# Layer 0's feed-forward input products as seven products of halves, the residual summed in DRAM, some low parts made on GpSimd

## The chip, the cores and the metric

One core of a Trainium2 chip runs the whole program. The metric is device time in microseconds (us) of one execution; several executions are taken and their median is given. The engines are TensorE (PE in the profile, its weight loads PEld), VectorE (DVE), ScalarE (ACT), GpSimd (POOL) and SyncE (SP, which here only issues transfers). POOL issues transfers too.

## The reference

One inference step of two layers over 640 tokens (512 latent, 128 context), model width 1024, in float32. Layer 0 mixes by attention, layer 1 by a bidirectional mLSTM; each mixer is followed by a SwiGLU feed-forward block with 2816 hidden columns. Shift, scale and gate of every block come from a product of the conditioning with `w_ada`. What the change touches is the feed-forward block:

```python
D_MODEL = 1024
D_FF = 2816

def modulate(x, g, shift, scale):
    return rms_norm(x, g) * (1.0 + scale) + shift

def swiglu(h, w_in, w_out):
    a, b = jnp.split(h @ w_in, 2, axis=-1)
    return (jax.nn.silu(a) * b) @ w_out

for l in range(2):
    ...                       # mixer: x = x + gate1 * mixer(modulate(x, ...))
    x = x + gate2 * swiglu(modulate(x, g_ffn[l], shift2, scale2), w_ffn_in[l], w_ffn_out[l])
y = rms_norm(x, g_final)
```

## The kernel before

**Numbers in two parts.** Every float32 operand of a large product is split into a high part (`hi`, rounded to the fp32r type) and a low part (`lo` = value - `hi`). A product is then three passes: high by high, high by low, low by high. ACT makes the high parts (`S.copy`), DVE the low parts (`V.tensor_tensor(... subtract)`).

**Weights.** `wspecs` lists all weight blocks in the order of use. `wload` takes the next one and starts its transfer into a buffer of the tag `raw` (four of them, shared with the modulation weights), `wprep` makes `whi` on ACT and `wlo` on DVE (five buffers each), `take` hands a pair to a product, `done` lets the next loads and preparations go. So weights are prepared up to five blocks ahead.

**Feed-forward, layer 0 (`ffn`).** For each of 22 blocks of 128 hidden columns PE makes `ffa` and `ffb` (the two halves of `h @ w_in`): 8 chunks of the model width x 3 passes x 2 halves of the tokens = 48 matmuls of 320 columns each, so 96 for a block. ACT and DVE make silu(a) * b and its high and low part `gh`, `gl`. Blocks go in groups (`GROUPS`: 8, 8, 6); after each group `ffn_out` multiplies the group's columns with `w_ffn_out` (tiles `fo`, 5 token tiles x 2 halves of the width) and `residual` adds gate * product onto x, which stays in SBUF.

**Feed-forward, layer 1 (`ffn7`).** The product of two 2 x 2 block matrices is made with seven products in place of eight. A unit is two blocks of 128 columns; the token dimension is halved (320 and 320), the model width too (512 and 512). The input appears in seven forms (`f1`, `f2`, `t1`, `t2`, `t3`, `f3`, `t4`: sums and differences of halves, class `Forms`), the weights in seven (steps 0 to 6; step 2 and step 4 load a block and add another onto it by an accumulating transfer of POOL's queue, steps 3 and 5 add on DVE). A unit is 7 products of 24 matmuls; results `X`, `Y`, `Z`, `W` (tiles `ffx`, `ffy`, `ffz`, `ffw`) are added into a and b on DVE. `put` writes the high and low parts of silu(a) * b into `g`. Units go in groups of 3, 3, 3 and 2, each followed by `ffn_out`.

**Modulation.** The product with `w_ada` for later blocks is made on DVE in the background: `ada_gen` loads a block of `w_adaT` (`araw`) and makes two dots (`junk`, L264, one for the latent and one for the context conditioning). `half_ada` is one dot, `bg_ada(1)` two. `ADA_FFN` says how many go after each block of layer 0's feed-forward. 160 dots in all.

**Order.** Each engine works through its instructions in program order, as the scheduler of the language laid them out; waits are semaphores. All tiles of one `tag` share their buffers.

Of the kernel before, what the change touches and what calls it, by code (L numbers as in the profile page):

```python
# [17 lines left out]
NT = 5  # L18
# [8 lines left out]
ADA_FFN = [0] + [2] * 8 + [1] * 13  # L27
# [18 lines left out]
GROUPS = [(0, 8), (8, 16), (16, 22)]  # L46


SEVEN = {1}
GROUPS7 = [(0, 6), (6, 12), (12, 18), (18, 22)]  # L50
# [3 lines left out]
def order7(d0, d1):  # L54

    us = range(d0 // 2, d1 // 2)
    steps = [(u, n) for u in us for n in range(7)]
    if d0 == 0:
        first = [(u, n) for u in (0, 1) for n in (0, 1)]
        steps = first + [s for s in steps if s not in first]  # L60
    return steps
# [8 lines left out]
def _build(ctx, tc, nc, A):  # L70
# [10 lines left out]
    xs_dram = dp.tile([TOK, 1024], F32, name="xs_dram", tag="xs")  # L81
    m_dram = dp.tile([64, TOK], F32, name="m_dram", tag="md")
# [63 lines left out]
    stp = cp.tile([128, 2, 2, 2, 3, 129], F32, name="stp", tag="stp")  # L146
    G.memset(stp.rearrange("p a e d k c -> p (a e d k c)"), 0.0)


    def wspecs():  # L150
# [11 lines left out]
        for l in range(2):  # L162
# [7 lines left out]
            for d0, d1 in GROUPS7 if l in SEVEN else GROUPS:  # L170
                if l in SEVEN:
                    st = {u: {"u": A["ffs"][u], "own": u != 1} for u in range(d0 // 2, d1 // 2)}
                    for u, step in order7(d0, d1):
                        yield st[u], step
                else:
                    for d in range(d0, d1):
                        for ab in range(2):
                            yield A["ffi"][l, d][:, ab]
                for half in range(2):
                    yield from chunk(A["ffo"][l, half][:, d0:d1, :], d1 - d0)  # L180
# [5 lines left out]
    ready = []  # L186
    live = [0]

    def wload():
# [4 lines left out]
        if isinstance(src, tuple):  # L194
# [3 lines left out]
            if first:  # L198

                raw = st[step] = (cp.tile([128, 2, 4, 128], F32, name=nm("wr"), tag=f"cB{step}") if step < 2 and st["own"] else  # L200
                                  Wp.tile([128, 2, 4, 128], F32, name=nm("wr"), tag="raw", bufs=4))
                SP.dma_start(raw, st["u"][first])
# [5 lines left out]
        SP.dma_start(raw, src)  # L208
# [3 lines left out]
    def wprep(n=99):  # L212
        for _ in range(min(n, len(raws))):
            if n == 99 and live[0] - len(raws) >= HELD:
                break
            raw = raws.pop(0)
# [10 lines left out]
            V.tensor_tensor(out=lo, in0=raw, in1=hi.bitcast(F32), op=ALU.subtract)  # L227
# [245 lines left out]
    class Forms:  # L473
# [14 lines left out]
        def split(self, name, f, cols, neg=False):  # L488
# [24 lines left out]
        def second(self, f, g, cols):  # L513
# [21 lines left out]
    def ffn7(l, x, forms, norm_last, bg, gate_fn, tile_done):  # L535
        gate = None
# [21 lines left out]
        def put(s, b, i, half):  # L558
            V.tensor_tensor(out=s, in0=s, in1=b, op=ALU.mult)
            for c, n, o in ((0, 256, 256 * half), (256, 64, 512 + 64 * half)):  # L560
# [3 lines left out]
                V.tensor_tensor(out=lo, in0=src, in1=hi.bitcast(F32), op=ALU.subtract)  # L564
# [15 lines left out]
        def step(u, n, i):  # L580
            w = units.setdefault(u, {})
            if n == 0:
                w["X"] = one("ffx")
                product(w["X"][0], 0, True, False)
                if u == 0:
                    norm_last()
                w["a1"] = T(640, "a1")
                S.copy(v2(w["a1"]), w["X"][1][0][1])
            elif n == 1:
                Y = two("ffy")  # L590
                product(Y[0], 1, True)
                a1 = w.pop("a1")
                add(a1, a1, Y)
# [16 lines left out]
            elif n == 5:  # L610
# [3 lines left out]
                put(silu(a2), w.pop("b2"), i, 1)  # L614
            else:
# [1290 lines left out]
```

## Time and profile before

| what | us |
|---|---|
| median of 3 runs | 1640.87 (1639.44 to 1643.06) |
| profiled execution, its own time | 1635.13 |
| its span, first to last instruction | 1633.4 |
| PE busy / DVE / ACT / POOL | 1592.5 / 1112.0 / 747.7 / 181.6 |
| layer 0's mixer up to its second half | 0 to 376 |
| second half of its output product | 376 to 399.5 |
| feed-forward of layer 0 | 399.5 to 870 |
| mLSTM mixer of layer 1 | 870 to 1165 |
| second half of its output product | 1165 to 1190.5 |
| feed-forward of layer 1 | 1190.5 to 1633.4 |

The stages are cut where the first matmul of a stage starts. The span is what the engines did in one execution; the execution's own time has some 1.7 us around it.

### The profile page before, as it was taken

The page shows a single profiled execution, that of the slowest core. Times are in us where ns is not written, and L with a number is a line of the kernel's source. Part 1 is how long each engine was busy: PE and PEld are TensorE (multiplying, and loading weights), DVE is VectorE, ACT ScalarE, POOL GpSimd, SP SyncE. Part 2 cuts the span into 40 slices and gives each one's busy share as a digit, 9 for nine tenths or more (in the row PEclk, how much of TensorE's full clock was granted, in tenths as well). Part 3 has the DMA queues.
Part 4 walks back from the last instruction along what each step waited for, and adds up shares of the span by engine and source line. Part 5 has one row for each costly group of instructions (what it writes and reads, how often), then busy time and mean ns, then how long its engine had stood idle before and what let it go on. Part 6 is the DMA issues. An engine that isn't in the chain of part 4 may idle for free.

```text
span 1633.4 us, 24402 instructions
## 1 busy us (share of the span) xinstructions
PE 1592.5 (97%) x9434; PEld 1447.0 (89%) x9434; DVE 1112.0 (68%) x1924; ACT 747.7 (46%) x1546; POOL 181.6 (11%) x213
## 2 busy tenths in 40 slices
PE   8999999999999999999999999989999999999997
PEld 7877898788999799979989998988789899899896
DVE  7687888866665565435557638598698677577567
ACT  5442558946432133213336234666476245155153
POOL 0001103420000000000000002663100100000000
PEclk8999999999999999999999999989999999999999
DMA  8354030043444343313324516452436554364331
GB/s 330 144 175 158 31 101 26 5 153 98 133 150 143 99 160 113 107 52 129 117 94 139 172 50 203 158 152 92 110 104 162 130 131 140 78 168 130 79 102 65
DMA packets 60900, 199.38 MB, mean 122 GB/s; under 512 B 7696, under 2 KB 10512, under 8 KB 60784
## 3 DMA queue, kind: packets, MB, share of 16 engines
q1 hardware_dynamic: 52736, 170.84, 32.6%
q0 software_dynamic: 7904, 26.79, 7.1%
q8 instruction: 74, 1.21, 0.3%
q14 instruction: 42, 0.34, 0.1%
q10 hardware_dynamic: 144, 0.20, 0.0%
HBM read 191.09 MB, written 6.71 MB: 121 GB/s over the span
## 4 chain that ended last, share of the span: by engine, by line
PE 87%; DVE 5%; ACT 4%; DMA 2%; issue 1%; POOL 0%; SPq 0%; DVEq 0%; POOLq 0%; ACTq 0%
PE ffa L343 9%; PE ffb L343 9%; PE fo L323 6%; PE fo L321 6%; PE fo L322 6%; PE ffw L546 5%; PE ffx L546 5%; PE ffz L546 4%; PE qk L343 3%; PE ffy L546 2%; PE in L321 2%; PE in L323 2%; PE in L322 2%; PE s L1133 2%; PE vo L323 2%; PE vo L322 2%
## 5 line engine op out<-in xcount | busy, mean ns | idle before, releaser
L226 ACT CAST whi<-wr 128x1024 fp32r<-128x1024 f32 (+2 forms) x228 | 235.2, 1034 | 539.9 <-PE fo L323 150.9
L227 DVE TENSOR_TENSOR wlo<-wr,whi 128x1024 fp32r<-128x1024 f32 (+2 forms) x228 | 275.0, 1212 | 147.5 <-ACT whi L226 145.4
L264 DVE SCALAR_TENSOR_TENSOR junk<-araw,cB 128x1024 bf16<-128x1024 f32 x160 | 194.8, 1245 | 28.6 <-DMA araw<-w_adaT 28.4
L456 DVE TENSOR_TENSOR tmp<-fo,g 128x512 f32<-128x512 f32 (+1 forms) x71 | 48.4, 682 | 110.3 <-PE fo L323 100.5
L321 PE MATMUL fo<-whi,hh 128*128 128x512 f32 x220 | 88.2, 401 | 0.0
L323 PE MATMUL fo<-whi,hl 128*128 128x512 f32 x220 | 87.9, 399 | 0.0
L323 PE MATMUL fo<-whi,g 128*128 128x512 f32 (+1 forms) x224 | 86.9, 390 | 0.0
L322 PE MATMUL fo<-wlo,g 128*128 128x512 f32 (+1 forms) x224 | 86.9, 388 | 0.0
L322 PE MATMUL fo<-wlo,hh 128*128 128x512 f32 x220 | 86.7, 394 | 0.0
L321 PE MATMUL fo<-whi,g 128*128 128x512 f32 (+1 forms) x224 | 86.6, 387 | 0.0
L343 PE MATMUL ffa<-hh,whi 128*128 128x320 f32 (+1 forms) x352 | 82.0, 310 | 0.0
L343 PE MATMUL ffa<-hl,whi 128*128 128x320 f32 (+1 forms) x352 | 81.8, 310 | 0.0
L343 PE MATMUL ffa<-hh,wlo 128*128 128x320 f32 (+1 forms) x352 | 81.5, 309 | 0.0
L343 PE MATMUL ffb<-hh,whi 128*128 128x320 f32 (+1 forms) x352 | 81.1, 308 | 0.2 <-ACT hh L375 0.2
L343 PE MATMUL ffb<-hl,whi 128*128 128x320 f32 (+1 forms) x352 | 80.7, 307 | 0.3 <-DVE hl L376 0.3
L343 PE MATMUL ffb<-hh,wlo 128*128 128x320 f32 (+1 forms) x352 | 80.5, 306 | 0.0
L546 PE MATMUL ffx<-form,whi 128*128 128x320 f32 x352 | 78.0, 309 | 0.0
L546 PE MATMUL ffz<-form,whi 128*128 128x320 f32 x352 | 78.0, 308 | 0.0
L1081 ACT ACTIVATE P<-s,s 128x640 f32<-128x640 f32 (+1 forms) x80 | 56.9, 712 | 33.4 <-DVE s L1076 29.1
L322 PE MATMUL vo<-wlo,hh 128*128 128x384 f32 (+2 forms) x200 | 70.2, 351 | 2.0 <-DVE wlo L227 2.0
L323 PE MATMUL vo<-whi,hl 128*128 128x384 f32 (+2 forms) x200 | 70.3, 352 | 0.0
L321 PE MATMUL vo<-whi,hh 128*128 128x384 f32 (+2 forms) x200 | 70.1, 353 | 0.0
(420 smaller groups left out, 4152.0 us busy)
## 6 DMA issues: line engine op xcount, KB each, us to landing
araw<-w_adaT SPq DMA_DIRECT2D x80, 512.0 KB, 4.1
wr<-ffs SPq DMA_DIRECT2D x55, 512.0 KB, 3.8
wr<-ffi SPq DMA_DIRECT2D x44, 512.0 KB, 3.6
wr<-ffo SPq DMA_DIRECT2D x44, 512.0 KB, 3.6
wr<-ffs POOLq DMA_DIRECT2D x22, 512.0 KB, 6.6
D<-m_dram SPq DMA_DIRECT2D x16, 320.0 KB, 5.0
ada<-w_ada SPq DMA_DIRECT2D x9, 512.0 KB, 9.8
wr<-winvo SPq DMA_DIRECT2D x12, 384.0 KB, 3.4
```

The source lines that it names most:

```text
L226: S.copy(hi, raw)
L227: V.tensor_tensor(out=lo, in0=raw, in1=hi.bitcast(F32), op=ALU.subtract)
L264: V.scalar_tensor_tensor(out=junk, in0=w, scalar=1.0, in1=cB[c], op0=ALU.mult, op1=ALU.mult, accum_out=vecs[l][:, j, m, c:c + 1])
L321: PE.matmul(ps, sh, mh, start=first, stop=False)
L322: PE.matmul(ps, sh, ml, start=False, stop=False)
L323: PE.matmul(ps, sl, mh, start=False, stop=last)
L343: PE.matmul(ps, w_(kc), h_[:, kc, sl], start=(kc == 0 and i == 0), stop=(kc == nkc - 1 and i == 2))
L456: V.tensor_tensor(out=tmp, in0=ps, in1=gate[:, 0 if t < 4 else 1, cols], op=ALU.mult)
L546: PE.matmul(outs[e], w_[:, e, k, :], f_[:, k, :], start=(start and k == 0 and i == 0), stop=(stop and k == 3 and i == 2), skip_group_check ...
L1081: S.activation(out_p, S_ps, AF.Exp, bias=mx, accum_out=l)
L1133: PE.matmul(sps[:, p, 0:320], qa[0:96, tok], ka[0:96, p * 320:(p + 1) * 320], start=True, stop=True)
```

## The change

- Layer 0 uses `ffn7` too. `ffn`, `GROUPS` and `second_half` go. Layer 0's groups are 3, 2, 3 and 3 units; the forms of its input are made in the second half of its mixer's output product (`second_half7`).
- The residual no longer stays in SBUF during the feed-forward. `second_half7` stores x to `xa_dram`; in all groups but the last, `resid` makes tmp = gate * product on DVE and POOL's queue adds it onto `xa_dram` by an accumulating transfer; before the last group's output product ten transfers bring x back, and DVE adds there as before. Both layers do so. The SBUF buffer that x had holds the step-0 and step-1 weights of the units (`own`).
- Low parts made on POOL: those of step 4's weights, those of `g` in every unit but a group's last, and form t3 with its difference.
- In layer 0, norm and transposes of the last token tile (`norm_last`) come after the second product; layer 1's first order is (0,0), (0,1), (1,0).
- The dots are spread anew (`ADA_FFN`, `bg0`, `half_ada` near the end of attention): 56 before layer 0's feed-forward (50 until now), 80 in it (66), 24 in the mLSTM mixer (44).
- `load` keeps the weight transfers of SP's queue in program order. `stp` is filled with zeros at the start of layer 1's mixer.

```diff
-ADA_FFN = [0] + [2] * 8 + [1] * 13
-GROUPS = [(0, 8), (8, 16), (16, 22)]
-SEVEN = {1}
-GROUPS7 = [(0, 6), (6, 12), (12, 18), (18, 22)]
+ADA_FFN = [(u, n) for u in (1, 2) for n in (1, 2, 4, 6)] + [(u, n) for u in range(3, 8) for n in (2, 4, 6)][:14]
+GROUPS7 = [[(0, 6), (6, 10), (10, 16), (16, 22)], [(0, 6), (6, 12), (12, 18), (18, 22)]]
...
+    xa_dram = [dp.tile([TOK, 1024], F32, name=f"xa_dram{l}", tag=f"xa{l}") for l in range(2)]
...
+    def load(raw, src):
+        if loads:
+            with tc.issue_after(loads[-1]):
+                i = SP.dma_start(raw, src)
+        else:
+            i = SP.dma_start(raw, src)
+        loads[:] = [i.ins]
...
-            V.tensor_tensor(out=lo, in0=raw, in1=hi.bitcast(F32), op=ALU.subtract)
+            (G if isinstance(src, tuple) and src[1] in (4,) else V).tensor_tensor(out=lo, in0=raw, in1=hi.bitcast(F32), op=ALU.subtract)
...
-            V.tensor_tensor(out=g[0], in0=g[0], in1=g[1], op=ALU.subtract)
-            self.split("t3", g[0], cols)
             self.split("f3", g[1], cols, True)
+            G.tensor_tensor(out=g[0], in0=g[0], in1=g[1], op=ALU.subtract)
+            self.split("t3", g[0], cols, eng=G)
...
-                V.tensor_tensor(out=lo, in0=src, in1=hi.bitcast(F32), op=ALU.subtract)
+                (V if last else G).tensor_tensor(out=lo, in0=src, in1=hi.bitcast(F32), op=ALU.subtract)
...
+            for u, n in order7(l, d0, d1):
+                step(u, n, 2 * u - d0, 2 * u + 2 == d1)
+                if l == 0 and (u, n) in ADA_FFN:
+                    bg_ada(1)
...
+        def resid(ps, t, half, c0=0, c1=512):
+            cols = slice(half * 512 + c0, half * 512 + c1)
+            at = xa_dram[l][t * 128:(t + 1) * 128, cols]
+            tmp = T(c1 - c0, "tmp")
+            V.tensor_tensor(out=tmp, in0=ps, in1=gate[:, 0 if t < 4 else 1, cols], op=ALU.mult)
+            if final:
+                V.tensor_tensor(out=x[:, t, cols], in0=tmp, in1=x[:, t, cols], op=ALU.add)
+            else:
+                G.dma_start(at, tmp, accum_op=ALU.add)
+        if final:
+            for half in range(2):
+                for t in range(NT):
+                    cols = slice(half * 512, (half + 1) * 512)
+                    G.dma_start(x[:, t, cols], xa_dram[l][t * 128:(t + 1) * 128, cols])
...
+            G.dma_start(xa_dram[l][t * 128:(t + 1) * 128, :], x[:, t, :])
...
-    ffn(0, x, nl, hh, hl, lambda l, d: bg_fill() if d is None else bg_ada(ADA_FFN[d]), lambda: load_gate(0, 5), tile_done0)
+    def bg0(t):
+        if t % 2 == 0 and own7[0] is not None:
+            bg_ada(1)
+    ffn7(0, forms, nl, bg0, lambda: load_gate(0, 5), tile_done0)
```

DVE at the end of layer 0's first group, before: the last two blocks' work and the first output tiles (`mg` is x).

```order
L679 TENSOR_TENSOR sil_5187<-sil_5187,ffa_5185 128x640
L264 SCALAR_TENSOR_TENSOR junk_5307,vecs_102<-araw_5303,cB_100 128x1024
L264 SCALAR_TENSOR_TENSOR junk_5311,vecs_102<-araw_5309,cB_99 128x1024
L680 TENSOR_TENSOR sil_5187<-sil_5187,ffb_5186 128x640
L227 TENSOR_TENSOR wlo_5300<-wr_5297,whi_5299 128x1024
L682 TENSOR_TENSOR hl_4250<-sil_5187,hh_4249 128x640
L456 TENSOR_TENSOR tmp_5343<-fo_5318,g_5315 128x512
L457 TENSOR_TENSOR mg_1388<-tmp_5343,mg_1388 128x512
```

The same place of the change, the end of unit 2 (L587 adds a product from PSUM, L566 and L570 finish silu and its product, L575 makes a low part of `g`).

```order
L238 TENSOR_TENSOR wlo_5100<-wr_4975,whi_5099 128x1024
L587 TENSOR_TENSOR al_5013<-al_5013,ffw_5023 128x320
L570 TENSOR_TENSOR sil_4929<-sil_4929,al_5013 128x640
L238 TENSOR_TENSOR wlo_5136<-wr_5021,whi_5135 128x1024
L566 SCALAR_TENSOR_TENSOR sil_5089<-sil_5089,a_1219_5087 128x640
L575 TENSOR_TENSOR g_4299<-sil_4929,g_4298 128x2x256
L570 TENSOR_TENSOR sil_5089<-sil_5089,b_1207_5015 128x640
L275 SCALAR_TENSOR_TENSOR junk_5142,vecs_104<-araw_5140,cB_101 128x1024
L575 TENSOR_TENSOR g_4299<-sil_5089,g_4298 128x2x256
L575 TENSOR_TENSOR g_4299<-sil_5089,g_4298 128x2x64
L275 SCALAR_TENSOR_TENSOR junk_5144,vecs_104<-araw_5140,cB_102 128x1024
L653 TENSOR_TENSOR tmp_5168<-fo_5149,g_5146 128x512
```

The group's last lows, which the output product waits for, stand behind the unit's adds and a dot; the residual add behind `tmp` is gone.

POOL in layer 0's feed-forward, before: nothing but the gate's transfers between the mixer's loads and the store of x.

```order
L461 DMA xr_4162<-x 128x512
L291 DMA gd_5047<-grow_5045 16x128
L316 DMA g_5315<-gd_5047 128x8x128 x2
L291 DMA gd_7752<-grow_7750 16x128
L1372 DMA xs_dram<-mg_1388 128x1024 x5
```

POOL in the change, from unit 4's weights on: the step-4 low of unit 4, the lows of unit 3's `g`, weight loads, and the accumulating transfers of the second output product.

```order
L215 DMA wr_5580<-ffs 128x1024
L238 TENSOR_TENSOR wlo_5697<-wr_5580,whi_5696 128x1024
L575 TENSOR_TENSOR g_4299<-sil_5647,g_4298 128x2x256
L575 TENSOR_TENSOR g_4299<-sil_5647,g_4298 128x2x64
L575 TENSOR_TENSOR g_4299<-sil_5501,g_4298 128x2x256
L575 TENSOR_TENSOR g_4299<-sil_5501,g_4298 128x2x64
L215 DMA wr_5929<-ffs 128x1024
L657 DMA xa_dram_79<-tmp_5988 128x512
L215 DMA wr_6068<-ffs 128x1024
L657 DMA xa_dram_79<-tmp_6010 128x512
```

POOL's queue, empty there until now, holds the lows and the transfers in one line; the accumulating weight loads stand between them.

PE at the start of the change's layer 0: the end of the second product (`ffy`), the last tile's transposes (`nt`), and the first matmuls of the third (`ffz`, form t1 in `form_4012`).

```order
L557 MATMUL ffy_4333<-form_4011,whi_4208 128x320 x2
L557 MATMUL ffy_4333<-form_4011,wlo_4209 128x320
L425 MATMUL nt_4358<-ident,xn_4293 128x128 x4
L425 MATMUL nt_4368<-ident,xn_4295 128x128 x4
L557 MATMUL ffz_4403<-form_4012,whi_4224 128x320
L557 MATMUL ffz_4404<-form_4012,whi_4224 128x320
```

Two products stand ahead of the transposes, and the product behind them reads a form that is made from them.

## Rows read from the trace of the kernel before

**Rows 1.** The page, busy time of each engine with its share and instructions.

```profile
PE 1592.5 (97%) x9434; PEld 1447.0 (89%) x9434; DVE 1112.0 (68%) x1924; ACT 747.7 (46%) x1546; POOL 181.6 (11%) x213
```

**Rows 2.** Stretches by stage: length, busy us (instructions) by engine, granted clock, DMA share, GB/s.

```profile
376.00:399.50 23.50, 23.50 (x115) 19.19 (x114) 13.94 (x29) 15.69 (x40) 1.61 (x3) 1.00 0.11 37
399.50:870.00 470.50, 469.50 (x2816) 436.84 (x2815) 263.79 (x372) 158.01 (x225) 5.05 (x8) 1.00 0.37 119
870.00:1165.00 295.00, 287.04 (x1735) 262.20 (x1734) 203.51 (x430) 145.62 (x421) 86.31 (x98) 0.98 0.46 139
...
1190.50:1633.40 442.90, 428.90 (x2539) 399.86 (x2537) 316.70 (x427) 200.28 (x287) 22.00 (x25) 0.99 0.44 118
```

**Rows 3.** Finer stretches, same columns: eight blocks; first group; output product; three units.

```profile
571.42:683.64 112.22, 112.22 (x769) 112.20 (x768) 62.22 (x83) 39.40 (x48) 0.00 (x0) 1.00 0.41 131
...
1190.50:1274.30 83.80, 79.38 (x524) 78.62 (x522) 72.72 (x104) 52.71 (x80) 4.24 (x5) 0.96 0.52 139
1274.30:1315.80 41.50, 41.50 (x182) 33.69 (x181) 24.09 (x34) 8.01 (x11) 4.29 (x6) 1.00 0.43 101
1315.80:1389.73 73.93, 73.93 (x505) 73.91 (x504) 54.51 (x69) 42.14 (x53) 2.74 (x4) 1.00 0.54 150
```

**Rows 4.** PE's waits in layer 0's feed-forward: total us, times, longest.

```profile
PE nt L414 <- DVE xn L402: 0.5, 2, 0.3
PE ffb L343 <- DVE hl L376: 0.3, 1, 0.3
```

**Rows 5.** PE's waits in the first group of layer 1.

```profile
PE nt L414 <- DVE xn L402: 3.8, 1, 3.8
```

**Rows 6.** PE's waits in the mLSTM mixer.

```profile
PE ho L1664 <- DVE hs L1678: 4.0, 2, 2.1
PE vo L322 <- DVE wlo L227: 2.0, 1, 2.0
```

**Rows 7.** DVE's timeline in a unit of layer 1: start, us, instruction.

```profile
1456.91 0.82 DVE L559 TENSOR_TENSOR sil<-sil,b 128x640 f32<-128x640 f32 x1
1457.65 0.82 DVE L559 TENSOR_TENSOR sil<-sil,al 128x640 f32<-128x640 f32 x1
1458.42 1.70 DVE L564 TENSOR_TENSOR g<-sil,g 128x512 fp32r<-128x512 f32 x4
1460.03 2.35 DVE L227 TENSOR_TENSOR wlo<-wr,whi 128x1024 fp32r<-128x1024 f32 x2
```

**Rows 8.** Timeline in the mLSTM mixer, DVE's dots beside a product on POOL.

```profile
1012.24 1.21 DVE L264 SCALAR_TENSOR_TENSOR junk<-araw,cB 128x1024 bf16<-128x1024 f32 x1
...
1013.38 1.21 DVE L264 SCALAR_TENSOR_TENSOR junk<-araw,cB 128x1024 bf16<-128x1024 f32 x1
...
1013.69 1.79 POOL L1583 TENSOR_TENSOR og<-og,ph 128x384 f32<-128x384 f32 x1 [3.33 <-ACT og L134]
...
1014.53 2.03 DVE L264 SCALAR_TENSOR_TENSOR junk<-araw,cB 128x1024 bf16<-128x1024 f32 x1
```

**Rows 9.** POOL's groups by form: count, busy us, mean ns, idle before.

```profile
L1699 POOL TENSOR_TENSOR hs<-hs,og 128x512 f32<-128x512 f32 x7 | 8.9, 1274 | 0.4
...
L1623 POOL TENSOR_TENSOR ph<-kn,D 128x256 f32<-128x256 f32 x8 | 5.0, 620 | 1.2 <-ACT D L1548 1.2
...
L1768 POOL TENSOR_TENSOR hs<-hs,gfin 128x768 f32<-128x768 f32 x1 | 1.8, 1796 | 54.5 <-ACT s L392 54.5
```

**Rows 10.** POOL's timeline while DVE did nothing.

```profile
1040.03 1.02 POOL L1583 TENSOR_TENSOR og<-og,ph 128x384 f32<-128x384 f32 x1 [1.26 <-ACT og L134]
```

**Rows 11.** DVE's waits in layer 0's feed-forward: total us, times, longest.

```profile
DVE junk L264 <- DMA araw<-w_adaT: 14.0, 8, 3.2
```

**Rows 12.** Transfers by line: issuing queue, count, KB each, median us to landing.

```profile
wr<-ffs POOLq DMA_DIRECT2D x22, 512.0 KB, 6.6
...
xs_dram<-mg POOLq DMA_DIRECT2D x5, 512.0 KB, 2.9
xr<-xs_dram POOLq DMA_DIRECT2D x10, 256.0 KB, 4.4
```

More of the change, by code (lines that the diff above doesn't have):

```diff
@@ L169, in wspecs @@
                 yield from chunk(A["w_oab" if l == 0 else "w_oc"][half], 8)
[L170 to L178, printed above, removed]
+            for d0, d1 in GROUPS7[l]:
+                st = {u: {"u": A["ffs"][l, u], "n": u, "l": l} for u in range(d0 // 2, d1 // 2)}
+                for u, step in order7(l, d0, d1):
+                    yield st[u], step
                 for half in range(2):
@@ L198, in wload @@
             if first:
-                raw = st[step] = (cp.tile([128, 2, 4, 128], F32, name=nm("wr"), tag=f"cB{step}") if step < 2 and st["own"] else
-                                  Wp.tile([128, 2, 4, 128], F32, name=nm("wr"), tag="raw", bufs=4))
-                SP.dma_start(raw, st["u"][first])
+                u = st["n"]
+                if step > 1 or st["n"] + st["l"] == 0 or (st["l"], u, step) == (1, 1, 0):
+                    raw = Wp.tile([128, 2, 4, 128], F32, name=nm("wr"), tag="raw", bufs=4)
+                elif u == 0:
+                    raw = cp.tile([128, 2, 4, 128], F32, name=nm("wr"), tag=f"cB{step}")
+                else:
+                    place = 2 * (u % 2) + step
+                    if own7[0] is None:
+                        own7[0] = L("own")
+                    raw = own7[0][:, place * 1024:(place + 1) * 1024].rearrange("p (d k c) -> p d k c", d=2, c=128)
+                st[step] = raw
+                load(raw, st["u"][first])
                 if second:
@@ L556, in silu, with put @@
             return s
-        def put(s, b, i, half):
+        def put(s, b, i, half, last):
             V.tensor_tensor(out=s, in0=s, in1=b, op=ALU.mult)
@@ L578, in ffn7, with step @@
         units = {}
-        def step(u, n, i):
+        def step(u, n, i, last):
             w = units.setdefault(u, {})
@@ L1306, in begin0 @@
         nat(acc0[t], mh, ml, t, ch, 0)
+        half_ada()
     def step0(t):
@@ L1312, in f @@
             qs[t] = ssq0(x[:, t, :])
-            if t == order[1]:
+            if t in order[:2]:
                 half_ada()
@@ L1742, in _build, with tile_done1 @@
     NW[0] = 8
-    forms, nl = second_half7(vecs[1], gate, xs_dram, x)
+    forms, nl = second_half7(1, gate, xs_dram, x)
     gfin = None
     dst = lambda t: A["o_ys"][t * 128:(t + 1) * 128, :] if t < 4 else A["o_yp"]
-    def tile_done1(t, half, c0=None):
+    def tile_done1(x, t, half, c0=None):
         nonlocal gfin
```

120 lines of the change are left out of this document (40 added, 80 removed).

## Prediction

> **What bounds the kernel now.** I read the page's table of engines first: TensorE (PE) is busy for 97% of the span, VectorE (DVE) for 68%, GpSimd (POOL) for 11% [rows 1]. A share over the whole span says little where stages differ, so the stretches come next [rows 2]. The reader is to see that PE is full in every stage and that the two feed-forward stages do the same job in two ways: layer 0 takes 470.5 us, layer 1 takes 442.9 us with a tail of about 10 us in it, and DVE works 264 us in the first and 317 us in the second. The finer stretches [rows 3] give the price of a product. In layer 0 eight blocks of 128 hidden columns are 768 matmuls in 112.22 us, 0.1461 us each. In layer 1 three units are 504 matmuls in 73.93 us, 0.1467 us each, all at a granted clock of 1.00. PE's waits in layer 0's stage are only at its start and below a microsecond [rows 4]; in layer 1's first group there is one of 3.8 us for a norm that DVE makes late [rows 5]; the mLSTM stage has 4.0 us and 2.0 us behind DVE [rows 6]. So fewer matmuls are worth their full time, as long as DVE keeps pace.
>
> **What it removes on PE.** 22 blocks of 96 matmuls are 2112, at 0.1461 us 308.6 us. Eleven units of seven products of 24 are 1848, at 0.1467 us 271.1 us. That is **-37.5 us**. The output products are the same in number.
>
> **What it asks of DVE.** Layer 0 now carries the work of the seven-product form and 80 dots for the modulation vectors (66 before). DVE's price is the spacing of its instructions in a full stretch, since each starts before the one ahead is recorded as done: two 1024-column lows take 2.35 us, so 1.13 each; a group of two 512- and two 128-column lows takes 1.70 us, so 0.8 for a pair; a 640-column product 0.74 us [rows 7]; dots start 1.15 us apart [rows 8]. I count the rows of DVE in the instruction order of the changed kernel between the last tile before a group of units and the last low of `g`, which the output product waits for: 15 dots in group 1 (units 0 to 2), 13 in group 2 (units 3, 4), 18 in group 3 (units 5 to 7), 2 in group 4, and 32 beside the output products. The layer-1 stretch of three units needs 54.51 us of DVE and its first group, with the norm forms in it, 72.72 us [rows 3].
>
> - Group 1: 72.7 + 15 x 1.15, less 3 x 1.13 (a step-4 low moved to POOL in each unit), less 4 x 0.8 (lows of `g` of two units), less 4 x 0.6 (t3 of two tiles) = 81 us. PE has 73.9 us of products, and 2.8 us more until the first output tile needs the last unit (two thirds of a tile of 4.15 us, ten to 41.5 us [rows 3]): 76.7 us.
> - Group 2: two thirds of 54.5 + 13 x 1.15 - 2 x 1.13 - 1.6 = 47 us, against 49.3 + 1.4 = 50.7 us.
> - Group 3: 54.5 + 18 x 1.15 - 3.4 - 3.2 = 68.6 us, against 76.7 us.
> - Group 4: 54.5 + 2.3 - 6.6 = 50 us, against 76.7 us.
>
> So DVE's own work alone is too much only in group 1; dropping the residual add (0.6 us a tile) gives room only beside the output products, where DVE already waits for PE.
>
> **What POOL takes, and what it costs DVE.** A POOL low of 512 columns takes 1.27 us alone, 256 take 0.62 and 768 take 1.80 [rows 9]. No row has 1024 or 128; on that line they are estimates of 2.35 us and 0.4 us. POOL then works 19 us in group 1 (three step-4 lows, four pairs of `g`, four t3 pieces), 8 us in group 2, 14 us in group 3. That fits POOL. It doesn't fit beside DVE for nothing. A product of 384 columns on POOL takes 1.02 us when DVE reads nothing [rows 10], but 1.79 us when it starts during a dot, and the next dot then takes 2.03 us in place of 1.21 [rows 8]: POOL waited for the first, the second waited for POOL, and DVE lost 0.82 us, 0.8 of what POOL's instruction takes alone. What DVE reads from PSUM is not held so (its adds of `ffx` to `ffw` and `tmp` read PSUM with one operand); by the order some 0.7 of DVE's time in these groups goes to instructions with two SBUF operands. I take 0.8 x 0.7 = 0.56 of POOL's time as lost on DVE, bounds 0 (every low falls beside a PSUM read) and 1.
>
> [...]
>
> **The sum of waits.** Group 1: 81 + 0.56 x 19 = 91.6 us; DVE also stands idle early, since tile 3's norm goes DVE, ACT, PE, DVE in turn (11 us of DVE idle in layer 1's first group: 83.8 - 72.7 [rows 3]); in layer 0 only two products, 7 us, stand ahead of those transposes and the third needs them, and I take 4 us. 95.6 - 76.7 = **19 us** of PE waiting, 4 of it at the first t1 product and the rest at the group's first output tile. Group 2: 47 + 4.5 = 51.8, **1 us**. Group 3: 68.6 + 7.8 = 76.4, **0**. Dots also wait for their weights: 14.0 us for 66 dots now [rows 11], 17 for 80; what falls in full stretches I take as a quarter, **4 us**, bounds 0 and 10. Together 24 us. Layer 0's old start loses about 1 us that goes. Layer 1's first group: 72.7 - 9 + 0.56 x 19 = 74 us on DVE, as before, **0** (bounds -3 and +10); its other groups need 54.5 - 6.6 + 7.8 = 56 us of 73.9. The mLSTM stage loses 20 dots, 23 us of DVE; its PE waits are 6 us, of which I take **-2 us**, bounds -5 and 0. The second half of layer 0's mixer gains forms and six dots ahead of it, **+1 us**, bounds 0 and 4.
>
> **What is hidden.** Thirty accumulating transfers of `tmp` a layer: the nearest row is a plain 512 KB store of 2.9 us, the other end the accumulating weight load of 6.6 us [rows 12]. Nobody reads `xa_dram` until the last group, so they cost nothing unless a held `tmp` buffer stops DVE; POOL issues them in its own time beside the output products, where nothing else but a weight load and one low stands in its queue. The ten loads of x before the last output product wait for the buffer of `own`, free two products into the last unit, so they have some 14 us and four PSUM tiles of 4.15 us behind them; with their cover gone, a landing of 4.4 us once a layer [rows 12]. Weight loads that accumulate are issued behind the lows of the unit before and needed over 30 us later.
>
> **Sum.** -37.5 + 24 - 1 - 2 + 0 + 1 = -15.5 us. The profiled execution took 1635.13 us with a span of 1633.4; it would be 1619.6. The median of the runs is 1640.87, 5.7 above that execution, so I forecast 1625 us.
>
> **Rivals.**
> - *DVE keeps pace.* The lows fall beside PSUM reads and ACT and the prepared weights (five ahead) absorb the rest; waits of 4 us at the start of layer 0 alone: -37.5 + 4 - 3 + 1, 1605 us. For it: layer 1 runs without a wait after its first product at 74% DVE. Against it: 81 us of DVE in group 1.
> - *The gain is eaten in place.* A loss share of 0.8, as on the dots of [rows 8], in every low: by the same sums group 1 waits 24 us, groups 2 and 3 3 each, layer 1's first group 6, dots 5. That is 41 us against 37.5 and the small terms, within 0.2% of before, 1642 us.
> - *Slower: POOL's lock holds all of DVE.* At a share of 1, group 1 waits 81 + 19 + 4 - 76.7 = 27 us, group 2 47 + 8 - 50.7 = 4, group 3 68.6 + 14 - 76.7 = 6, layer 1's first group 63.7 + 19 + 11.1 - 83.8 = 10, dots 5: 52 us, so -37.5 + 52 - 3 + 1 = +12, 1653 us. It decides from a share of some 0.8 up. For it: rows 8 show it on the very instructions that are added; against it: a quarter or more of DVE's time reads PSUM.
> - *The saving is not there* can be ruled out: the count of matmuls is fixed and layer 1 shows their rate.
>
> **How the numbers follow.** Forecast case 0.43 (1613 to 1637), DVE keeps pace 0.27, eaten 0.13, lock 0.17. The range from 1603 to 1650 leaves out part of the lock case and the edge of the best one; the forecast case alone is 1613 to 1637. 0.2% is 3.3 us, about what this kernel's measurement can tell from no change: faster (below 1637.6) 0.70, same 0.13, slower 0.17.
>
> **What would show it.** Right: 77 products in layer 0 of 3.52 us each; a wait of 10 to 20 us of PE at the first output tile of layer 0's group 1 that ends on DVE's `g`; DVE at 90% or more over groups 1 to 3; dots and lows of 2 to 3.5 us beside POOL's lows; no new wait in layer 1. Wrong: no wait at that place; or waits in every group; or PE waiting for a weight low made on POOL or for x.

## Result: slower by 1%

The changed kernel took 1657.78 us (median of 4 runs, 1656.74 to 1660.75) against 1640.81 us before (4 runs): a ratio of 1.0105, 95% interval 1.0087 to 1.0123. The forecast was 1625 us, the range ended at 1650. The profiled execution has a span of 1655.0 us; the working of the forecast, 1633.4 - 15.5, gives 1617.9, so 37.1 us have to be explained.

The engines of the changed kernel, which answer to [rows 1]:

```profile
PE 1573.2 (95%) x9170; PEld 1420.4 (86%) x9170; DVE 1206.3 (73%) x1984; ACT 799.6 (48%) x1630; POOL 412.2 (25%) x415
```

PE is busy 19 us less than before, and the span is 22 us longer: PE waits. The stages of the changed kernel, columns as in [rows 2]:

```profile
405.10:882.50 477.40, 444.46 (x2552) 409.13 (x2551) 394.59 (x529) 207.41 (x303) 136.89 (x117) 0.96 0.66 186
882.50:1204.70 322.20, 312.57 (x1858) 281.54 (x1857) 194.34 (x426) 164.34 (x467) 84.84 (x110) 0.98 0.40 122
1204.70:1655.00 450.30, 431.65 (x2537) 399.52 (x2535) 298.86 (x354) 199.65 (x286) 124.47 (x108) 0.98 0.56 142
```

Taken at the first matmul of each stage, layer 0's feed-forward starts 5.4 us later (forecast +1), takes 6.9 us more (forecast -14.5), layer 1's mixer 1.7 us more (-2), layer 1's feed-forward with the tail 7.6 us more (0). More than half of the miss (21.4 of 37.1 us) lies in layer 0's feed-forward. PE's waits there, in place of [rows 4]:

```profile
PE ffz L557 <- DVE b L587: 17.7, 7, 4.5
PE fo L332 <- DVE al L587: 4.8, 1, 4.8
PE nt L425 <- DVE xn L413: 4.4, 3, 3.8
PE ffz L557 <- ACT form L505: 2.8, 1, 2.8
PE ffz L557 <- DVE form L506: 1.3, 1, 1.3
PE gT L298 <- DVE vecs L266: 1.2, 1, 1.2
```

The first row is the one that the forecast did not have: seven waits of PE's second product into a PSUM tile (`ffz`, step 5), for DVE's additions to `b` (L587), which must first have read that tile. They are spread over groups 1 to 3; 13.0 of the 17.7 us lie in groups 2 and 3. DVE's own waits in the stage, in place of [rows 11]:

```profile
DVE junk L275 <- DMA araw<-w_adaT: 25.9, 11, 6.6
DVE wlo L238 <- ACT whi L237: 18.7, 18, 3.0
...
DVE own L232 <- DMA wr<-ffs: 1.7, 2, 1.4
```

DVE stands 25.9 us at dots whose weights have not landed. The longest, at the end of group 1, on DVE and on SP's queue (start, us, instruction):

```profile
500.19 0.89 DVE L587 TENSOR_TENSOR b<-b,ffw 128x320 f32<-128x320 f32 x2
507.66 1.23 DVE L275 SCALAR_TENSOR_TENSOR junk<-araw,cB 128x1024 bf16<-128x1024 f32 x1 [6.59 <-DMA araw<-w_adaT]
...
509.96 0.82 DVE L587 TENSOR_TENSOR a<-al,ffz 128x640 f32<-128x640 f32 x1
```

```profile
499.45 0.33 SPq L186 DMA_DIRECT2D araw<-w_adaT  x1
499.82 1.12 SPq L186 DMA_DIRECT2D own<-ffs  x2
```

SP could issue the load only at 499.45, when a buffer came free; two more loads followed at once, and it landed some 8 us later. SP's loads wait for the readers of the four buffers, the lows and the dots themselves (groups 1 to 3: total us, times, longest):

```profile
SPq L186 <- DVE wlo L238: 119.7, 27, 24.4
SPq L186 <- DVE junk L275: 106.3, 34, 7.7
```

Behind that dot stood the last additions of the group, and PE waited 4.8 us at its first output tile. The row for that wait names an addition to `al`, which reads the PSUM tile `ffw`, and not a low of `g`: in the kernel `fo` and `ffw` take their PSUM buffers from the same four. DVE had nothing to do for 6.6 us: this is not an engine that is full.

Columns as in [rows 2]: group 3's products, where DVE is busy for 69.57 of 78.60 us; that wait at the end of group 1, and the stretch behind it; a wait of 4.5 us for `b` in group 3, and the stretch behind that:

```profile
633.00:711.60 78.60, 71.57 (x466) 70.59 (x465) 69.57 (x87) 38.72 (x51) 29.79 (x20) 0.96 0.73 198
507.30:512.40 5.10, 0.26 (x3) 0.04 (x1) 4.74 (x8) 1.50 (x3) 0.00 (x0) 0.78 0.35 116
512.40:516.00 3.60, 3.60 (x9) 2.83 (x10) 3.57 (x6) 2.35 (x5) 0.00 (x0) 0.50 0.59 196
650.60:655.60 5.00, 0.53 (x4) 0.27 (x3) 5.00 (x7) 0.63 (x2) 0.87 (x1) 0.79 0.98 179
655.60:659.00 3.40, 3.40 (x13) 3.40 (x14) 3.40 (x6) 1.05 (x1) 0.00 (x0) 0.50 0.98 311
```

The last four rows show a second price of a wait: behind each wait the granted clock is 0.50, and in the last row 13 matmuls take 3.40 us in place of 1.9 at a clock of 1.00 (0.146 us each, [rows 3]). Six stretches of this stage have a clock of 0.50, 34.1 us together, and each begins during a wait of PE of 2.4 to 4.8 us or within 0.9 us of its end. The price in the stage is about 11.9 us: PE is busy 444.46 us at a mean granted clock of 0.96, and 432.58 us at 0.99 with the same matmuls in run e16 below, where it waits for 9.5 us. By the trace's clock records 25.4 us of PE's work in the stage ran at 0.50, and 3.7 us in e16; if work takes twice as long at half of the clock, the price is half of that difference, 10.9 us, an estimate.

Layer 1's first group, in place of [rows 5]:

```profile
PE ffz L557 <- ACT form L505: 2.9, 1, 2.9
PE nt L425 <- DVE xn L413: 2.8, 1, 2.8
PE ffz L557 <- DVE b L587: 1.9, 1, 1.9
PE ffz L557 <- DVE form L506: 1.0, 1, 1.0
```

8.6 us against 3.8. And what POOL's lows did, by form (count, busy us, mean ns):

```profile
L238 POOL TENSOR_TENSOR wlo<-wr,whi 128x1024 fp32r<-128x1024 f32 x22 | 60.6, 2757 | 171.1 <-ACT whi L237 150.6 <-DVE al L587 20.3
L570 DVE TENSOR_TENSOR sil<-sil,b 128x640 f32<-128x640 f32 x22 | 36.8, 1674 | 0.0
L570 DVE TENSOR_TENSOR sil<-sil,al 128x640 f32<-128x640 f32 x22 | 29.1, 1321 | 0.1
```

The product of two SBUF operands that takes 0.82 us alone [rows 7] takes 1.67 and 1.32 us on average. Over layer 0's stage DVE's instructions beside a low of POOL took some 35 us longer than the median of their kind without one. POOL's 43 instructions for the low parts there (the two differences for t3 among them) add up to 78.4 us.

### The profile page after: what moved, and what is told of

Read it like the earlier page. It is cut to its first block, busy times and chain, and to the rows that moved or that the text cites. A ratio compares the mean times of both kernels' runs of the same rounds, so it can differ in the third digit from the quotient of the medians.

```text
span 1655.0 us, 24531 instructions
## 1 busy us (share of the span) xinstructions
PE 1573.2 (95%) x9170; PEld 1420.4 (86%) x9170; DVE 1206.3 (73%) x1984; ACT 799.6 (48%) x1630; POOL 412.2 (25%) x415
## 4 chain that ended last, share of the span: by engine, by line
PE 71%; DVE 13%; ACT 6%; DMA 5%; issue 4%; POOL 1%; DVEq 0%; SPq 0%; POOLq 0%; ACTq 0%
PE ffz L557 8%; PE ffx L557 6%; PE ffw L557 6%; PE fo L332 5%; PE fo L334 5%; PE fo L333 5%; PE qk L354 3%; PE ffy L557 3%; DVE wlo L238 2%; PE in L332 2%; PE vo L334 2%; PE vo L333 2%; PE in L334 2%; PE vo L332 2%; PE in L333 2%
## 5 line engine op out<-in xcount | busy, mean ns | idle before, releaser
L557 PE MATMUL ffz<-form,whi 128*128 128x320 f32 x704 | 166.3, 325 | 27.6 <-DVE b L587 19.7
L332 PE MATMUL fo<-whi,g 128*128 128x512 f32 (+1 forms) x444 | 176.3, 398 | 5.1 <-DVE al L587 4.8
L333 PE MATMUL fo<-wlo,g 128*128 128x512 f32 (+1 forms) x444 | 174.1, 393 | 0.0
L334 PE MATMUL fo<-whi,g 128*128 128x512 f32 (+1 forms) x444 | 174.0, 394 | 0.0
L557 PEld LDWEIGHTS ffz<-form,whi 128*128 128x128 f32 x704 | 125.4, 200 | 31.7 <-DVE b L587 22.3
L238 DVE TENSOR_TENSOR wlo<-own,whi 128x1024 fp32r<-128x1024 f32 x78 | 105.6, 1354 | 37.0 <-ACT whi L237 35.9
L237 ACT CAST whi<-own 128x1024 fp32r<-128x1024 f32 x78 | 81.6, 1046 | 103.9 <-PE ffz L557 40.9
L557 PEld LDWEIGHTS ffx<-form,whi 128*128 128x128 f32 x704 | 118.1, 188 | 0.8
L557 PE MATMUL ffz<-form,wlo 128*128 128x320 f32 x352 | 113.2, 322 | 0.0
L557 PE MATMUL ffx<-form,wlo 128*128 128x320 f32 x352 | 109.0, 310 | 0.0
L332 PEld LDWEIGHTS fo<-whi,g 128*128 128x128 f32 x444 | 84.1, 189 | 25.7 <-DVE al L587 5.1
L334 PEld LDWEIGHTS fo<-whi,g 128*128 128x128 f32 x444 | 83.8, 189 | 19.8
L333 PEld LDWEIGHTS fo<-wlo,g 128*128 128x128 f32 x444 | 83.9, 189 | 19.1 <-DVE wlo L238 0.4
L575 POOL TENSOR_TENSOR g<-sil,g 128x512 fp32r<-128x512 f32 (+1 forms) x56 | 76.6, 1404 | 14.0 <-ACT g L574 14.0
```

The lines of the kernel that those rows point to most:

```text
L237: S.copy(hi, raw)
L238: (G if isinstance(src, tuple) and src[1] in (4,) else V).tensor_tensor(out=lo, in0=raw, in1=hi.bitcast(F32), op=ALU.subtract)
L332: PE.matmul(ps, sh, mh, start=first, stop=False)
L333: PE.matmul(ps, sh, ml, start=False, stop=False)
L334: PE.matmul(ps, sl, mh, start=False, stop=last)
L557: PE.matmul(outs[e], w_[:, e, k, :], f_[:, k, :], start=(start and k == 0 and i == 0), stop=(stop and k == 3 and i == 2), skip_group_check ...
```

## The experiments

Four causes were tried against each other: A, DVE's queue order (what stands ahead of the additions to `b`); B, POOL's lows hold DVE; C, DVE has too much to do; D, DVE stands for transfers. Each run has its own runs of the kernel before beside it, which the ratio goes by. Lengths are of the profiled execution, from the first matmul of a stage to that of the next; stages that an edit does not touch differ by up to 4 us between these kernels, so less is not read from them.

| run | median us | ratio to before (95%) | L0 feed-forward | L1 mixer | L1 feed-forward, tail |
|---|---|---|---|---|---|
| before | 1640.8 | | 470.5 | 320.5 | 442.7 |
| after | 1657.8 | 1.0105 (1.0087 to 1.0123) | 477.4 | 322.2 | 450.3 |
| e1 lows on DVE | 1637.6 | 0.9969 (0.9955 to 0.9982) | 465.1 | 321.2 | 444.8 |
| e2 dots moved | 1679.8 | 1.0220 (1.0199 to 1.0241) | 493.0 | 323.4 | 452.5 |
| e3 no dots | 1636.4 | 0.9964 (0.9949 to 0.9979) | 455.9 | 321.6 | 452.3 |
| e4 dots without loads | 1646.5 | 1.0030 (1.0017 to 1.0042) | 461.8 | 321.6 | 452.2 |
| e5 no accumulating stores | 1654.7 | 1.0083 (1.0062 to 1.0103) | 471.8 | 324.4 | 451.7 |
| e6 an addition on POOL | 1654.6 | 1.0083 (1.0060 to 1.0106) | 475.0 | 326.9 | 450.3 |
| e7 short lows on DVE | 1647.7 | 1.0023 (1.0000 to 1.0047) | 469.9 | 321.4 | 452.1 |
| e8 thin | 1646.0 | 1.0036 (1.0018 to 1.0054) | 465.4 | 325.8 | 452.4 |
| e9 e1 + thin | 1640.3 | 1.0003 (0.9993 to 1.0013) | 461.8 | 325.9 | 444.7 |
| e10 e1 + no dots | 1620.7 | 0.9862 (0.9838 to 0.9887) | 450.3 | 323.5 | 443.4 |
| e11 dots' own buffer | 1688.4 | 1.0291 (1.0277 to 1.0305) | 503.0 | 324.1 | 453.0 |
| e12 e9, other start | 1639.6 | 1.0000 (0.9984 to 1.0016) | 466.8 | 327.2 | 445.0 |
| e13 ACT reads PSUM | 1657.7 | 1.0105 (1.0084 to 1.0126) | 475.3 | 324.5 | 450.3 |
| e14 e1 + ACT reads | 1630.8 | 0.9942 (0.9923 to 0.9960) | 457.5 | 323.6 | 444.0 |
| e15 e1 + pairs | 1622.3 | 0.9887 (0.9871 to 0.9904) | 447.3 | 325.5 | 444.1 |
| e16 e15 + ACT reads | 1618.9 | 0.9872 (0.9850 to 0.9895) | 442.1 | 325.3 | 443.9 |

**e1, e7: POOL's lows.**

```diff
-            (G if isinstance(src, tuple) and src[1] in (4,) else V).tensor_tensor(out=lo, ...)
+            V.tensor_tensor(out=lo, ...)
-                (V if last else G).tensor_tensor(out=lo, ...)
+                V.tensor_tensor(out=lo, ...)
-            G.tensor_tensor(out=g[0], in0=g[0], in1=g[1], op=ALU.subtract)
-            self.split("t3", g[0], cols, eng=G)
+            V.tensor_tensor(out=g[0], in0=g[0], in1=g[1], op=ALU.subtract)
+            self.split("t3", g[0], cols)
```

> All low parts that the change put on POOL go back to DVE, in both layers. Theory A (place in DVE's queue: PE's second products wait for DVE's add of `b`, which stands behind dots and weight lows): DVE gets some 2.3 us more to do per unit, part of it ahead of those adds, so layer 0's feed-forward stage grows from 477 us by 3 to 12 us; total 1660 to 1670 us. Theory B (POOL's lows hold DVE): DVE loses the instructions of 1.5 to 3 us beside POOL's lows, the stage shrinks by 5 to 15 us; total 1643 to 1653 us. Theory C (DVE has simply too much to do): longer by the whole added work of the full groups, 15 us or more.

20.2 us less than the changed kernel, so B holds and C in this form falls: DVE got some 26 us of instructions more in each layer's stage (11 x 1.13, 14 x 0.8 and 4 x 0.6 us at the forecast's prices), and the stages are shorter. In layer 0's stage DVE is even busy for less, 385.65 us in place of 394.59 (columns as in [rows 2]):

```profile
404.80:869.80 465.00, 440.94 (x2551) 406.67 (x2550) 385.65 (x572) 208.18 (x303) 59.70 (x74) 0.97 0.68 190
```

The products of two SBUF operands return to their length in e1:

```profile
L570 DVE TENSOR_TENSOR sil<-sil,al 128x640 f32<-128x640 f32 x22 | 18.0, 820 | 0.1
L570 DVE TENSOR_TENSOR sil<-sil,b 128x640 f32<-128x640 f32 x22 | 18.0, 818 | 0.0
```

e7 leaves the first pair of lines as in the changed kernel (the step-4 lows stay on POOL) and takes the rest of e1.

> Only the low parts of `g` and of t3 go back to DVE; the step-4 weight lows stay on POOL (all back on DVE gave 1637.6 us). If POOL's lows cost by their time (in layer 0 some 30 us of weight lows, 45 us of the others), three fifths of the 20 us come back: about 1646 us. If the short lows of `g` do the harm (they stand on the way of the output product and are made beside DVE's multiplications): about 1640 us. If the long weight lows do it (one of 2.8 us holds DVE longest): about 1654 us.

10.1 us of the 20.2 come back: long and short lows share the harm about evenly. The eleven long lows that stay on POOL in layer 0's stage lengthen DVE's instructions by some 18 us, where all of the lows do by 35. In layer 1 nothing came back (452.1 us).

**e2: other places for the dots.**

```diff
-ADA_FFN = [(u, n) for u in (1, 2) for n in (1, 2, 4, 6)] + [(u, n) for u in range(3, 8) for n in (2, 4, 6)][:14]
+ADA_FFN = [(u, n) for u in (1, 2) for n in (0, 4, 5, 6)] + [(u, n) for u in range(3, 8) for n in (4, 5, 6)][:14]
```

> The same 22 pairs of dots in the units, but those behind steps 1 and 2 stand behind steps 0, 4, 5 and 6, so that none lies between the product of step 2 and the adds of `b` in steps 3 and 4. Theory A (place): PE's waits for `b`, 17.7 us in layer 0, fall under 6 us, and the slow products behind them go too; total 1635 to 1645 us. Theory C (too much DVE work): the waits move to other places, total within 3 us of 1658. Theory D (transfers are late): the waits of the dots for their weights stay at some 26 us in the units and go on to `g` at the end of the groups; total 1650 to 1658.

22 us more: all three were wrong. PE's waits for `b` stayed (19.0 us), those at the groups' first output tiles grew from 4.8 to 12.8 us. DVE's own waits for transfers in the stage:

```profile
DVE junk L275 <- DMA araw<-w_adaT: 15.7, 10, 5.4
...
DVE own L232 <- DMA wr<-ffs: 8.6, 3, 3.8
```

DVE stands 8.6 us at additions for weights that POOL's queue adds, but less at the dots, so 24.3 us together against 27.6 (25.9 + 1.7) in the changed kernel: D does not explain this loss. Its instructions beside POOL's lows took some 42 us longer, 7 more than in the changed kernel; what makes up the rest is open. The scheduler decides where a dot stands among the others, so theory A as a rule of thumb on the code's places falls; but that places matter is plain, since the same dots at other places cost 22 us.

**e3, e4, e10: the dots' instructions and their loads.** e3 leaves out the dots of the 22 places and keeps their loads; e4 keeps the instructions on a resident row and leaves out the loads; e10 is e3 with the edit of e1.

```diff
                     load(raw, A["w_adaT"][l, j, m])
-                    ada_dot(l, j, m, raw, (0,))
+                    if not unit[0]:
+                        ada_dot(l, j, m, raw, (0,))
```

> The dots inside layer 0's units are left out, their weight loads stay (the modulation values of those dots are constants, so the output differs). Theories A and C: all waits for `b` and the one for `g` go, 22 us and some 9 us of slow products; total 1625 to 1632 us. Theory D in the form that the traffic itself delays the weights: still above 1650 us.

> The dots inside layer 0's units stay as instructions, but they read a resident row instead of a loaded one, so 22 loads of 512 KB and the waits for them are left out (the modulation values differ). Theory D (DVE's queue stands still at a dot whose weights are in flight, 26 us in these groups): the 4.8 us wait for `g` at the end of group 1 goes and the waits for `b` fall to some 8 us; total 1635 to 1645 us. Theory C (DVE's work): nothing changes beyond 4 us.

> All low parts on DVE and no dots in layer 0's units (their loads stay; the modulation values differ). If the two causes add, layer 0's stage falls from 477 to some 444 us (12.3 and 21.5 less) and the total to 1616 us; what is left above the 433 us of pure products and output products is the start (some 9 us). If they overlap: stage 452 us or more, total 1625 or more. This also shows what the seven-product form is worth with DVE out of the way.

Without the dots the stage is 21.5 us shorter, without their loads alone 15.6 us (its profiled execution took 1641.3 us, 5 less than its median: the medians give 21.4 and 11.3). So half or more of the dots' price goes with their loads, D, and the rest with their 1.15 us each. The traffic as such is not it, since e3 keeps the loads. But e4 also leaves the dots' places in the four buffers to other loads, and what that gives is not told apart from DVE's standing. The four corners of lows and dots, 477.4, 465.1, 455.9 and 450.3 us, show that the two reliefs add up in part: the lows on POOL cost 12.3 us beside the dots and 5.6 us without them.

**e5, e6: two smaller suspects.** e5 drops `G.dma_start(at, tmp, accum_op=ALU.add)`. e6:

```diff
-                    V.tensor_tensor(out=st[0], in0=st[0], in1=st[2], op=ALU.add)
+                    E = G if st["n"] + st["l"] == 0 else V
+                    E.tensor_tensor(out=st[0], in0=st[0], in1=st[2], op=ALU.add)
```

> The sixty accumulating stores of `tmp` into DRAM are left out (so the output lacks the residual part of three of four groups). Theory D2 (the transfers that the new residual adds make the weights of units and dots land late): the landing times of `own` (7.1 us) and the dots' waits for weights (41 us) fall clearly, total 1645 us or less. The other theories: nobody waits for these stores, total within 4 us of 1658.

> One addition of 1024 columns, the first of layer 0's first unit (step 0 + step 2 of its weights), goes from DVE to POOL. In the changed kernel DVE stands 5.1 us at this addition in the second half of layer 0's mixer, since the weights of step 2 get a buffer late and then land by two transfers, and the norm of the next tile is behind it. If that is why layer 0's feed-forward stage starts 5.4 us late, the start goes from 405.1 to about 401.5 us and the total to some 1654 us. If something else holds the start, it stays at 405 us and the total within 2 us.

Both give 3 us, with intervals that overlap that of the changed kernel. The residual in DRAM costs little, as forecast, though it is not shown to be free: the stage of e5's profiled execution is 5.6 us shorter. In e6 DVE's wait at that addition is gone, but PE still waits 2.9 us for the norm of the tile behind it, and the stage starts at 404.1 us: the wait moved on.

**e8, e9, e12, e11: fewer dots, and their buffers.** e8 thins them to 12 pairs, one dot at a time (`ADA_VO` puts ten pairs more in the mixer); e9 adds e1; e12 adds to e9 that layer 0's first group begins like layer 1's.

```diff
-ADA_FFN = ...
+ADA_FFN = [(u, n) for u in (1, 2) for n in (0, 1, 2, 3, 4, 6)] + [(u, n) for u in range(3, 9) for n in (0, 2)]
-ADA_VO = [1, 0, 1, 1]
+ADA_VO = [1, 1, 1, 1]
-                    bg_ada(1)
+                    half_ada()
```

> POOL's lows as in the changed kernel; 12 pairs of dots in the units in place of 22, one dot at a time with other work between, ten pairs more in layer 1's mixer. Leaving all 22 pairs out gave 21.5 us of layer 0's stage, about 1 us a pair. If the price is by the pair: 10 us less in the stage, some 2 to 4 us more in the mixer, total 1650 to 1652 us. If it is the bunching (two dots at a stretch, three or four pairs a unit, so that DVE falls behind by more than the one product that it may): stage 460 us or less, total 1640 to 1645 us.

> Both reliefs together: all low parts on DVE, and 12 pairs of dots in the units, one dot at a time, ten pairs more in layer 1's mixer. If POOL's hold and the crowded dots are two separate causes, their gains (20.2 and 11.8 us) add up: about 1626 us, below the kernel before. If they relieve the same waits, most of the second is lost: 1632 to 1638 us.

> As the run with all lows on DVE and thinned dots, and layer 0's first group begins as layer 1's does, with the first product of unit 1 as its third, so that PE has 3.5 us more to do before it needs the last norm's forms. If the start's waits (8.5 us in the changed kernel at the transposes and the first t1 product) are the lateness of that norm: 4 to 8 us less than that run. If the weight of that product holds one of the four buffers too long: weights come late, and no gain or a loss of up to 5 us.

e8 gained 11.8 us, e9 nothing over e1 (its mixer, with ten pairs more, is 4.7 us longer). DVE's waits in e9:

```profile
DVE wlo L238 <- ACT whi L237: 24.7, 28, 3.0
DVE own L232 <- DMA wr<-ffs: 18.2, 3, 7.4
...
DVE junk L275 <- DMA araw<-w_adaT: 5.0, 3, 3.0
```

DVE hardly stands at the dots any more, but it does at three additions, for 18.2 us. The reading, which e15 tests: a load whose two dots are apart holds one of the four `raw` buffers for longer, and the unit's own weights come late. e12's other order changed nothing that can be told (PE's wait for the norm grew from 3.8 to 7.7 us).

e11 is the changed kernel with the dots' weights in the free fifth of `own`:

```diff
-                    raw = Wp.tile([128, 1024], F32, name=nm("araw"), tag="raw", bufs=4)
+                    if own7[0] is not None:
+                        raw = own7[0][:, 4096:5120]
+                    else:
+                        raw = Wp.tile([128, 1024], F32, name=nm("araw"), tag="raw", bufs=4)
```

> The changed kernel, but the dots' weights in layer 0's units go to a buffer of their own (a free quarter beside `own`) in place of one of the four that the units' weights use. If DVE's standing at dots whose weights are in flight is the cost (some 26 us in the units; leaving the loads out gave 15.6 us of the stage): waits for `araw` under 10 us, total 1642 to 1650 us. If it is the dots' own 1.15 us each: total within 4 us of 1658.

The miss was complete, 30.6 us more, but it speaks for D. With one buffer a load can only start when the dots before it are done:

```profile
DVE junk L275 <- DMA own<-w_adaT: 40.9, 23, 3.4
DVE wlo L238 <- ACT whi L237: 19.7, 14, 3.6
DVE own L232 <- DMA wr<-ffs: 14.4, 2, 7.8
```

DVE stands 55.3 us for transfers (40.9 + 14.4) in place of 27.6 (25.9 + 1.7), and the stage is 25.6 us longer. That is not a price per us, though: DVE stands 16.4 us at the dots in e5, 17.4 in e13 and 15.7 in e2, all some 9 us less than in the changed kernel, and their stages are 5.6 us shorter, about as long and 15.6 us longer. DVE may stand less at a dot because it comes to it later.

**e13, e14: more slack for PE.**

```diff
+                w["b2"] = T(640, "b2")
+                for e, p in w["Z"][1]:
+                    S.copy(v2(w["b2"])[:, e], p)
...
-                add(w["b2"], al, w["Z"])
+                V.tensor_tensor(out=w["b2"], in0=w["b2"], in1=al, op=ALU.add)
...
-                add(w["b2"], w["b2"], w["W"])
+                wc = T(640, "wc")
+                for e, p in w["W"][1]:
+                    S.copy(v2(wc)[:, e], p)
+                V.tensor_tensor(out=w["b2"], in0=w["b2"], in1=wc, op=ALU.add)
```

> The changed kernel, but ACT copies the first products `ffz` and `ffw` out of PSUM as soon as they are made, and DVE adds the copies to `b` from SBUF; DVE's number of additions is the same. If the slack of one product is what turns DVE's lag into PE's waits: the waits of `ffz` for `b` (17.7 us in layer 0) fall under 5 us, part of them comes back as waits for `g` at the ends of groups 1 and 3, total 1640 to 1650 us. If DVE's total work sets the pace: all of it comes back, total within 4 us of 1658. If ACT is as late as DVE (it waits for DVE's `a` before the sigmoid, and its copies stand behind that): the waits become waits for ACT, 1655 us or more.

> The same copies by ACT, with all low parts on DVE (which alone gave 1637.6 us). Its waits for `b` are 8.5 us. By the slack theory: 1628 to 1633 us. By the total-work theory: 1637 us. By the theory of ACT as late as DVE: 1637 or more.

PE's waits in layer 0's feed-forward in e13:

```profile
PE fo L332 <- DVE al L587: 12.2, 3, 6.7
PE gT L298 <- DVE vecs L266: 5.9, 1, 5.9
PE nt L425 <- DVE xn L413: 4.1, 3, 3.6
PE ffw L557 <- ACT wc L622: 3.3, 1, 3.3
```

Not one wait for DVE's additions to `b` is left, and the time is the same: the waits moved, 12.2 us to the groups' first output tiles, 5.9 us to the gate (`gT`), 3.3 us to ACT's copies. The additions that now read SBUF alone keep their 0.82 us, so no new hold by POOL's lows hides a gain here. So in the changed kernel it is DVE's pace over a group that counts, and a wait's place need not be its cause; A in its form on `b` falls. With the lows on DVE the slack may be worth something (e14 against e1: 6.9 us in the medians, 4.4 by the ratios, with intervals that just touch).

**e15, e16: a version that beats both.** e1, 12 pairs of dots in the units with both dots together, ten pairs more in the mixer; e16 adds ACT's copies.

```diff
+ADA_FFN = [(u, n) for u in (1, 2) for n in (1, 3, 6)] + [(u, 3) for u in range(3, 9)]
+ADA_VO = [1, 1, 1, 1]
```

> All lows on DVE, 12 pairs of dots in the units (in place of 22), both dots of a pair together, so that a dot's weights hold one of the four buffers only briefly; ten pairs more in layer 1's mixer. The run with the halves of a pair apart gave 1640.3 us, with 18 us of DVE standing at an addition for late weights. If that holding of buffers was its cost: 1626 to 1632 us. If the number of dots in the mixer is the cost: 1638 or more.

> The same with ACT's copies of `ffz` and `ffw`. By the slack theory 3 to 6 us less than the run before it, some 1624 us; else the same.

e15 differs from e9 in that a pair's dots are together, and in their places: 18.0 us. DVE is busy as long (363.8 us in the stage, 364.0 in e9), but stands 5.6 us at the additions in place of 18.2. So it is not the amount of work; pairing and places are not told apart. e16's further 3.4 us lie within the intervals. Its stage, and PE's waits in it:

```profile
403.90:846.00 442.10, 432.58 (x2552) 400.42 (x2551) 362.14 (x519) 222.50 (x337) 59.32 (x74) 0.99 0.67 188
```

```profile
PE nt L425 <- DVE xn L413: 4.3, 3, 3.8
PE ffz L557 <- ACT form L505: 3.4, 1, 3.4
PE ffz L557 <- ACT b L611: 1.6, 1, 1.6
PE fo L332 <- ACT g L574: 0.2, 1, 0.2
```

28 us less than the stage before, and 21 us (1.3%) less in the whole: the seven products do pay once DVE has no lows to wait for and fewer dots to stand at. It still stands 14.8 us for transfers in this stage (7.4 at dots, 7.4 at additions to `own`), but PE hardly waits for it.

## Why the prediction was wrong

*What PE saves* was right. The forecast left 432 us for layer 0's stage without waits (470.5 - 37.5 - 1); e16 is busy for 432.58 us.

*The sum of waits* failed. It came to 24 us; the stage had 32.9 us of PE idle (477.40 - 444.46), and PE was busy 11.9 us longer than in e16, by the estimate above 10.9 of it through the low clock behind the waits, a term that the forecast did not have. These 8.9 and 11.9 us, with 0.6 from the line above, are the 21.4 us by which this stage missed. Inside the sum:

- "Dots also wait for their weights", a quarter of 17 us, **4 us** with bounds 0 and 10, was the mis-sized term. DVE stood 25.9 us at them, and 11 to 16 us go with their loads (e4). The forecast scaled the waits of the kernel before by the number of dots; but DVE's queue is in order, and a load starts only when a reader frees one of four buffers (in groups 1 to 3 SP's loads waited 106.3 us for dots and 119.7 us for lows).
- "Group 2: 1, group 3: 0" followed from adding instructions without the standing; the waits for `b` there are 3.5 and 9.5 us. Group 1's waits came to about the 19 us of the forecast, but 8.5 us at its start in place of 4, and 4.8 us at its first output tile in place of 15; that one ended on an addition and not on `g`. So the 19 us of group 1 were right by luck.
- *What POOL takes.* At the forecast's own prices POOL's part takes some 54 us in the stage (11 x 2.35, 14 x 1.67, 4 x 1.27), and 0.56 of it, 30 us, is lost on DVE. POOL's instructions took 78.4 us, held in their turn (a 1024-column low has a mean of 2.76 us, 2.39 at least), and DVE lost 35 us, 0.64 of the 54. So the loss was nearly right in size; what failed is the trade. The moved lows spare DVE 26 us, so it lost 9 us by being helped; the forecast counted this as about even, and e1 shows 20.2 us for both layers. Beside a low of 2.40 us a product of 0.82 us took 3.08 us (last section). What DVE reads from PSUM was not held, as forecast: the 19 additions of 320 columns (to `a` and `al`) that ran beside an instruction of POOL in this stage took 0.47 to 0.48 us, the others 0.47 to 0.49.

*Layer 1's first group, 0* (bounds -3 and +10) came to +4.5 us (88.3). With the lows on DVE it is 83.3 us, as before [rows 3]; by e1 5.5 of the 7.6 us of this stage are POOL's lows. The other 2 us were not traced, and their cause is open.

*Second half of layer 0's mixer, +1* (bounds 0 and 4) came to 5.4 us: one wait of 3.1 us for a norm behind an addition that stood 5.1 us for late weights, and slow products after it; e6 only moved it. *The mLSTM mixer, -2* was wrong in kind: its waits of 4.0 and 2 us [rows 6] are there unchanged with 20 dots fewer.

*What is hidden* held as far as the medians tell: the run without the residual transfers is 3 us faster, with intervals that overlap.

Of the rivals, the slower one (a share of 1; "lock" is its name for the holding in [rows 8], and no run shows what makes it) named half of the mechanism and came nearest, 1653 us; its condition, a share of 0.8, was not met (0.64), and its waits stood in other places; it was enough that the share made the trade a loss. The other half, DVE standing for its dots' weights, stood in no rival. "Waits in every group" was named as a sign of a wrong forecast, and it came for groups 1 to 3; "no new wait in layer 1", a sign of a right one, failed too.

## What to carry to other kernels

An in-order engine that makes background work should not stand at its queue's head for a transfer (25.9 us of DVE at its dots here): count buffers and ask when each load can start, and put the standing into the engine's need. Before work is moved to a helper that slows the engine it helps, compare what the move spares with what the helper holds up; here sparing 26 us cost 35. And a wait's place need not be its cause: give it slack, and see whether it goes or moves.

## What was not expected of the hardware

A wait of 5 us cost more than itself: the granted clock was 0.50 in the stretches of 3.4 and 3.6 us read behind two of them, with 13 matmuls in 3.40 us. With 32.9 us of waits in its stage PE was busy 11.9 us longer than in e16, with 9.5. And one product of two SBUF operands on DVE, of 0.82 us, took up to 3.08 us beside a low of POOL that started with it:

```profile
448.31 3.08 DVE L570 TENSOR_TENSOR sil<-sil,al 128x640 f32<-128x640 f32 x1
448.32 2.40 POOL L238 TENSOR_TENSOR wlo<-wr,whi 128x1024 fp32r<-128x1024 f32 x1 [18.32 <-ACT whi L237]
```
